# RMSNorm with repeated rows on one core: the last tile loaded by rows and stored in two halves

## Chip, cores and metric

One core of a Trainium2 chip. The metric is the device time of one execution in microseconds (us), as the median of several executions. A run's state is "slow" when its time is over 1.5% above the fastest run of the same kernel in the same call, otherwise "fast". The span of a profile is about 1.8 us shorter than the device time of the same run.

## The reference

```python
def reference(x, gamma):              # x: (8, 512, 2048) float32, gamma: (2048,)
    x_rep = np.repeat(x, 2, axis=1)   # each row twice
    rms = np.sqrt((x_rep ** 2).mean(axis=-1, keepdims=True) + 1e-6)
    return (x_rep / rms * gamma[None, None, :]).astype(np.float32)
```

4096 rows of 8 KB are read, and each normalised row is written twice: 33.6 MB in, 67.1 MB out.

## The kernel before

A tile `y` has 128 partitions, with 4 input rows (`K = 4`) and so 8 output rows (`K * R`, `R = 2`) in each. A load puts the 4 input rows into places 4 to 7; row k is normalised into place 2k and copied to 2k + 1. There are 8 tiles and 3 buffers, so load 7 waits for store 4.

```python
def load(i, eng, parts=1):
    y = rows.tile([P, K * R, D], f32, name="y")
    step = K // parts
    for k in range(0, K, step):
        at = K * (R - 1) + k
        eng.dma_start(out=y[:, at : at + step, :], in_=x_t[i, :, k : k + step, :])
    ys.append(y)

load(0, nc.scalar, parts=K)
# ... gamma, eps; loads 1 and 2, on nc.scalar
for i in range(ntiles):
    y = ys[i]
    for k in range(K):
        xk = y[:, K * (R - 1) + k, :]
        y0, y1 = y[:, R * k, :], y[:, R * k + 1, :]
        # ... tiles sq, ss, rms, rstd
        nc.scalar.activation(out=sq[:], in_=xk, func=Act.Square, accum_out=ss[:])
        nc.scalar.activation(out=rms[:], in_=ss[:], func=Act.Sqrt, scale=inv_d, bias=eps_t[:])
        nc.vector.reciprocal(out=rstd[:], in_=rms[:])
        nc.vector.scalar_tensor_tensor(out=y0, in0=xk, scalar=rstd[:], in1=gamma_b[:],
                                       op0=Alu.mult, op1=Alu.mult)
        if k == K - 1:
            nc.vector.tensor_copy(out=y1, in_=y0)
        else:
            nc.scalar.copy(out=y1, in_=y0)
    nc.sync.dma_start(out=out_t[i], in_=y.rearrange("p j d -> p (j d)"))
    if i >= 1 and i + 2 < ntiles:
        load(i + 2, nc.gpsimd)
```

Three queues feed the same 16 DMA engines: stores from SP (`nc.sync`), the first three loads from ACT (`nc.scalar`), loads 3 to 7 from POOL (`nc.gpsimd`, the "software" queue). A run is a stretch of bytes contiguous on both sides, moved as one piece. A load has 128 runs of 32 KB (4 adjacent rows), a store 128 of 64 KB; each engine gets 8 of them.

## Time and profile before

| | before |
|---|---|
| time, median of 3 runs | 244.24 us (244.11 to 244.63) |
| span of the profile | 242.7 us |
| one load run of 32 KB / store run of 64 KB on its engine | 1.213 / 2.418 us |
| load 7 landed, median engine / last engine | 202.0 / 204.1 us |
| store 6 landed, median engine / last engine | 216.5 / 218.5 us |
| DMA idle before the last store (15 of 16 engines) | 216.7 to 221.9 us |

The runs and the landings are from the trace's records of single transfers, where each of the 16 engines ends its share of a DMA with a 4-byte write to a semaphore. These records agree with the instructions' times to some 0.3 us: load 7's last engine ends at 204.1 us in the records, while the instructions see the load landed at 204.4. All times are from the start of the span.

From the page of the kernel before: the span, the engines' busy time, what the DMA moved, and the chain of work that ended last, by engine.

```profile
span 242.7 us, 307 instructions
...
DVE 88.9 (37%) x73; ACT 116.1 (48%) x122; POOL 5.3 (2%) x10
...
DMA packets 2740, 100.69 MB, mean 415 GB/s; under 512 B 305, under 2 KB 305, under 8 KB 305
...
DMA 74%; ACT 10%; DVE 5%; ACTq 1%; issue 1%; POOLq 0%; SPq 0%
```

DMA is the limit: 415 GB/s in the mean, and three quarters of the chain, while no compute engine is busy half the time. So this change looks for time where the DMA stands idle. The stretches table of the kernel before, near the end, shows where; its columns are the stretch, its length, the busy time and instructions of DVE, ACT and POOL, the clock, the DMA share and GB/s (a transfer counts whole in the stretch in which it starts, so a share can pass 1).

```profile
core 0: us, DVE busy (x) ACT busy (x) POOL busy (x), PEclk, DMA share, GB/s
...
204.00:213.00 9.00, 4.95 (x4) 8.50 (x10) 0.00 (x0) 1.00 1.07 466
213.00:217.00 4.00, 2.28 (x2) 3.84 (x5) 0.00 (x0) 1.00 0.64 279
217.00:221.00 4.00, 3.89 (x4) 1.90 (x1) 0.00 (x0) 1.00 0.00 0
221.00:225.00 4.00, 0.00 (x0) 0.00 (x0) 0.00 (x0) 1.00 1.22 524
```

The DMA thins out at 213 us, moves nothing from 217 to 221, and then carries the last store by itself. The chain of waits of the kernel before, in order of time (start, length, what), tells what it waited for:

```profile
132.22 34.69 DMA out_dram<-y
...
167.48 36.93 DMA y<-in_x_dram
...
204.43 2.01 ACT sq L71 x2
...
208.89 1.99 ACT sq L71 x2
210.87 3.59 ACT y L83 x2
...
214.89 2.35 DVE y L76
...
219.73 1.23 DVE y L81
```

Load 7 is on its way for 36.93 us, then ACT and DVE work through four rows until 220.96 us. Then the store is issued, as the timeline of the store queue shows (start, length of the issue, engine, line, operation):

```profile
221.02 0.33 SPq L84 DMA_DIRECT2D out_dram<-y  x1
```

Its first run starts at 221.9. So 16.6 us of compute stand between landing and store, and the rest of store 6 covers about 12 of them.

### The profile page before, as it was taken

How to read it: one execution, taken by the hardware profiler on the slowest of the kernel's cores; microseconds unless marked ns; L12 is line 12 of the kernel's file. 1: busy time of each engine (PE TensorE's matmuls, PEld its weight loads, DVE VectorE, ACT ScalarE, POOL GpSimd, SP SyncE). 2: the span in 40 equal slices, each digit the busy share in tenths (PEclk: the TensorE clock that was granted, in tenths of full speed). 3: DMA queues.
4: the chain of work that ended last, by engine and by line, in shares of the span. 5: the costliest groups of instructions: out<-in, count | busy, mean ns of one | idle time of the engine just before them, and what ended most of it. 6: DMA issues, size and time to landing. Idle time of an engine off the chain costs nothing.

```text
span 242.7 us, 307 instructions
## 1 busy us (share of the span) xinstructions
DVE 88.9 (37%) x73; ACT 116.1 (48%) x122; POOL 5.3 (2%) x10
## 2 busy tenths in 40 slices
DVE  0458557772000035900557007550085400864000
ACT  2994997990000079600994019920299103991000
POOL 4000000010000000000000000000000000000000
DMA  7999999999899999799799799799999898948794
GB/s 270 443 439 437 400 432 454 410 466 432 373 459 405 459 432 518 346 518 432 346 432 518 346 432 518 342 437 427 432 437 508 351 508 351 518 184 346 346 518 173
DMA packets 2740, 100.69 MB, mean 415 GB/s; under 512 B 305, under 2 KB 305, under 8 KB 305
## 3 DMA queue, kind: packets, MB, share of 16 engines
q1 hardware_dynamic: 1154, 67.12, 63.9%
q0 software_dynamic: 720, 20.97, 20.1%
q10 hardware_dynamic: 864, 12.58, 12.7%
q14 instruction: 2, 0.02, 0.0%
HBM read 33.56 MB, written 67.11 MB: 415 GB/s over the span
## 4 chain that ended last, share of the span: by engine, by line
DMA 74%; ACT 10%; DVE 5%; ACTq 1%; issue 1%; POOLq 0%; SPq 0%
DMA y<-in_x_dram 44%; DMA out_dram<-y 30%; ACT sq L71 6%; DVE y L76 4%; ACT y L83 4%; ACTq L52 1%; DVE y L81 1%; ACT rms L73 0%; DVE rstd L75 0%; POOLq L52 0%; SPq L84 0%; POOLq L112 0%
## 5 line engine op out<-in xcount | busy, mean ns | idle before, releaser
L71 ACT ACTIVATE sq<-y 128x2048 f32<-128x2048 f32 x32 | 59.7, 1866 | 95.6 <-DMA y<-in_x_dram 95.6
L76 DVE SCALAR_TENSOR_TENSOR y<-y,rstd,gamma_b 128x2048 f32<-128x2048 f32 x32 | 75.3, 2352 | 1.2
L75 DVE RECIPROCAL rstd<-rms 128x1 f32<-128x1 f32 x32 | 5.1, 160 | 129.8 <-ACT rms L73 129.8
L83 ACT COPY y<-y 128x2048 f32<-128x2048 f32 x24 | 44.6, 1889 | 2.4 <-DVE y L76 2.4
L81 DVE COPY y<-y 128x2048 f32<-128x2048 f32 x8 | 9.8, 1227 | 0.3
L73 ACT ACTIVATE rms<-ss,eps_t 128x1 f32<-128x1 f32 x32 | 9.4, 294 | 0.7
L52 POOL DMA_DIRECT2D y<-in_x_dram x5 | 2.8, 559 | 159.9 <-DMA out_dram<-y 111.8
L71 ACT ACTIVATION_READ_ACCUMULATOR sq<-y 128x1 f32 x32 | 6.0, 186 | 0.0
L71 ACT ACT_TABLE_LOAD x1 | 1.3, 1283 | 4.3 <-issue 4.3
L58 POOL PARTITION_BROADCAST gamma_b<-gamma_b x1 | 2.3, 2292 | 2.6 <-DMA gamma_b<-in_gamma_dram 2.6
L73 ACT ACT_TABLE_LOAD x1 | 1.3, 1283 | 0.0
L60 DVE MEMSET eps_t<- 128x1 f32 x1 | 0.1, 59 | 0.8 <-PEq L101 0.8
L101 POOL MEMSET const-float32-0.0<- 128x1 f32 x1 | 0.1, 99 | 0.2 <-issue 0.2
L101 POOL MEMSET const-bfloat16-1.0<- 128x1 bf16 x1 | 0.1, 101 | 0.0
L101 POOL MEMSET const-uint8-127<- 128x1 uint8 x1 | 0.1, 101 | 0.0
L101 POOL MEMSET const-float32-1.0<- 128x1 f32 x1 | 0.1, 98 | 0.0
## 6 DMA issues: line engine op xcount, KB each, us to landing
y<-in_x_dram POOLq DMA_DIRECT2D x5, 4096.0 KB, 35.6
y<-in_x_dram ACTq DMA_DIRECT2D x2, 4096.0 KB, 26.9
y<-in_x_dram ACTq DMA_DIRECT2D x4, 1024.0 KB, 7.8
out_dram<-y SPq DMA_DIRECT2D x8, 34.1
gamma_b<-in_gamma_dram SPq DMA_DIRECT2D x1, 8.0 KB
```

Of the source, the lines that this page charges most:

```text
L52: eng.dma_start(out=y[:, at : at + step, :], in_=x_t[i, :, k : k + step, :])
L58: nc.gpsimd.partition_broadcast(out_ap=gamma_b[:], in_ap=gamma_b[0:1, :])
L60: nc.vector.memset(eps_t, eps)
L71: nc.scalar.activation(out=sq[:], in_=xk, func=Act.Square, accum_out=ss[:])
L73: nc.scalar.activation(out=rms[:], in_=ss[:], func=Act.Sqrt, scale=inv_d, bias=eps_t[:])
L75: nc.vector.reciprocal(out=rstd[:], in_=rms[:])
L76: nc.vector.scalar_tensor_tensor(out=y0, in0=xk, scalar=rstd[:], in1=gamma_b[:], op0=Alu.mult, op1=Alu.mult,)
L81: nc.vector.tensor_copy(out=y1, in_=y0)
L83: nc.scalar.copy(out=y1, in_=y0)
L101: nc = _bacc.Bacc("TRN2", target_bir_lowering=False, num_devices=1)
```

## The change

The intent is to close that gap: compute on row 0 before row 3 has landed, and store the first half while the second is computed.

```diff
+    def store(i, k0, k1):
+        nc.sync.dma_start(
+            out=out_t[i, :, R * k0 * D : R * k1 * D],
+            in_=ys[i][:, R * k0 : R * k1, :].rearrange("p j d -> p (j d)"),
+        )
@@
-        nc.sync.dma_start(out=out_t[i], in_=y.rearrange("p j d -> p (j d)"))
+            if i == ntiles - 1 and k % 2 == 1:
+                store(i, k - 1, k + 1)
+        if i < ntiles - 1:
+            store(i, 0, K)
         if i >= 1 and i + 2 < ntiles:
-            load(i + 2, nc.gpsimd)
+            load(i + 2, nc.gpsimd, parts=K if i + 2 == ntiles - 1 else 1)
```

Load 7 becomes four DMAs of 8 KB runs, 32 runs on each engine; store 7 becomes two DMAs of 32 KB runs. The built order of ACT's work on the last tile also changes. Before: Square of rows 0, 1, 2, copies of rows 0 and 1, Square of row 3, copy of row 2. After: Square of rows 0 and 1, copy of row 0, Square of rows 2 and 3, and only then the copies of rows 1 and 2. (The small square roots are left out here.)

## The prediction

> **What bounds the kernel now.** The DMA. The page shows 415 GB/s over the 242.7 us span and a chain of waits that is 74% DMA; ACT is busy 48%, DVE 37%. The DMA's only large idle stretch is near the end: in the stretches table it moves 279 GB/s at 213-217 us, nothing at 217-221, and then runs full. Timeline and chain: load 7 lands at 204.4, the four rows of the last tile compute until 220.96, store 7 is issued at 221.0 and its first packet moves at 221.9. Store 6 has ended by about 216.5 on 15 engines, 218.5 on a lagging one. So 3.5 to 5.5 us could be won.
>
> **How the queues share the engines.** In the trace's packets, load 7 (8 runs of 32 KB per engine, 1.213 us each) alternates one for one with store runs of 64 KB (2.418 us). The Trainium skill, DMA: Bandwidth & Descriptors, section Queues, rings and completion order, has each engine round-robin between queues by packet, typically 9-17 descriptors. This trace agrees on the round robin but shows turns of one run; even the 4-byte semaphore write waits a turn.
>
> **What the change does.** Load 7 becomes 32 runs of 8 KB, 0.309 us each (first tile's loads), so 9.89 us instead of 9.70: +0.2. Its share per turn beside a 64 KB store falls from 33% to 11%. Counting turns from 172.5 (load 6 done): six runs of store 5 end at 188.5 with 6 load runs moved; alone until store 6 starts at about 191.7, 15 moved (row 0 landed at 189.5); row 1 lands at about 197; eight runs of store 6 end at about 213.2 with 22 moved; the rest moves alone, row 2 at 213.9, row 3 at 216.5, on the lagging engine about 2 us later: row 3 at 218.7, instead of the whole load at 204.4. The load now ends when stores 5 and 6 end, not 14 us before.
>
> **Why the first half store doesn't fill the gap.** In the built instruction order ACT copies the second output of rows 1 and 2 after the Square of row 3, which waits for row 3's load. So the first half store waits for the load that lands last: 218.7 + 0.4 + Square 1.9 + copy 1.85 = 222.9 issue, first packet 0.9 later at 223.8 (before: 221.9). The second half (row 3: rms, rstd, scale 2.35, copy 1.23) is issued at about 229, hidden under the first half's 9.7 us. Then 19.4 us of data and 1.4 us of tail: span 244.6. Gain: the time from landing to the first store packet falls from 17.5 to 5.1 us; cost: landing is 14.3 later. Net +1.9.
>
> **Predicted time: 246.0 us (+0.7%), range 243.7 to 247.9.** Chances: faster by over 2% 0.04, within 2% 0.89, slower by over 2% 0.07.
>
> **What would show it.**
> - Row 3's load lands at 216-219 us; row 0 near 190; rows 1 and 2 far apart (about 197 and 214).
> - Store 5 ends some 5 us earlier than 195; store 6 about 213 instead of 216.5.
> - First half store issued 3.5-4.5 us after row 3 lands, after its Square and a copy; DMA idle gap of about 5 us still there, some 2 us later.
> - Everything before 167 us unchanged.
>
> **What would make it wrong.** If several 8 KB runs go in one turn, the load lands near 204-210, the half stores queue behind store 6, the gap closes and the span is about 239. If short software-queue descriptors cost more than 0.31 us, or the lagging engine (1.9 us here) lags more, it is slower.

## The result, and the profile after

| | before | after |
|---|---|---|
| time, median of 4 runs each | 244.44 us | 246.79 us (246.52 to 246.96) |
| ratio of the fast runs | | 1.0095, 95% interval 1.0076 to 1.0114 |
| span | 242.7 us | 244.9 us |
| last load landed, median / last engine | 202.0 / 204.1 | 216.8 / 219.0 us |
| store 6 landed, median / last engine | 216.5 / 218.5 | 216.0 / 217.2 us |
| (first) store of the last tile issued | 221.0 | 223.2 us |
| time per engine that no record covers, from 205 us to the last byte, mean of 16 | 5.4 us | 7.2 us |
| last byte moved | 241.4 | 243.7 us |

A ratio is the mean time of one kernel's fast runs over that of the other's in the same rounds, so it is not quite the ratio of the medians quoted here.

From the page of the kernel after, the same lines as before:

```profile
span 244.9 us, 317 instructions
...
DVE 89.1 (36%) x73; ACT 116.3 (48%) x122; POOL 6.9 (3%) x13
...
DMA packets 3316, 100.69 MB, mean 411 GB/s; under 512 B 369, under 2 KB 369, under 8 KB 369
...
DMA 76%; ACT 8%; DVE 4%; another core or an unknown queue 2%; ACTq 2%; issue 1%; POOL 0%; POOLq 0%; SPq 0%
```

The same bytes, moved at 411 instead of 415 GB/s. The stretches table of the kernel after:

```profile
204.00:213.00 9.00, 0.00 (x0) 1.22 (x1) 0.00 (x0) 1.00 0.93 400
213.00:217.00 4.00, 2.52 (x2) 1.08 (x3) 0.00 (x0) 1.00 0.89 381
217.00:221.00 4.00, 0.00 (x0) 1.62 (x1) 0.00 (x0) 1.00 0.03 12
221.00:225.00 4.00, 0.00 (x0) 4.00 (x5) 0.00 (x0) 1.00 0.31 131
```

The DMA is busier ahead of 217 us (381 instead of 279 GB/s in the four us before), and the gap has moved back rather than closed: 12 GB/s at 217 to 221, and still only 131 at 221 to 225. The chain of waits of the kernel after:

```profile
168.60 43.15 DMA y<-in_x_dram
...
211.78 2.01 ACT sq L77 x2
...
214.11 5.25 another core or an unknown queue
...
219.38 2.00 ACT sq L77 x2
221.38 1.79 ACT y L89
223.17 1.80 ACTq L121
...
225.40 2.36 DVE y L82
...
227.78 1.23 DVE y L87
```

The load is on the chain for 43.15 us up to row 2, and the next 5.25 us ("another core or an unknown queue") are the wait for row 3: the chain doesn't name that DMA, but the same wait stands in ACT's timeline as 5.27 us on the load. ACT had finished row 1's Square at 196 us, yet its copy of row 1 comes only after row 3's Square, at 221 us. (The 1.80 us of `ACTq L121` are the second of two copies; ACT's timeline has both as one piece of 3.68 us.) The store queue's timeline:

```profile
223.20 0.33 SPq L56 DMA_DIRECT2D out_dram<-y  x1
...
229.07 0.33 SPq L56 DMA_DIRECT2D out_dram<-y  x1
```

The second half is issued at 229.07, while the first still moves (until 233.9), and in the records the engines then run on without a pause to 243.7. So the work on row 3, with which the chain ends, cost no time: the chain follows the store issued last and doesn't show that it queued behind the first half.

Counting in the records how many runs start in steps of about one turn shows what became of the load. All 16 engines together; in both kernels store 5 moves at first:

```
before, step 1.21 us        load 32 KB  store 64 KB
 174.6                          15          0
 175.8                           1         15
 177.0                           0          1
 178.2                          15          0
 179.4                           1         15
after, step 0.91 us         load 8 KB   store 64 KB
 174.6                           7          2
 175.5                           9         13
 176.4                           0          1
 177.3                           7          2
 178.2                           9         13
 ...   (store 5 has ended, store 6 has not begun)
 190.1                          46          0
 191.0                          48          0
```

One run of the load, one run of the store, whatever their lengths. Before, the load gets 1.213 of every 3.63 us. After, it gets 0.309 of every 2.73 us, 11%. Only in the pause between store 5 and store 6 does it have the engines to itself.

### The profile page after: what moved, and what is told of

The parts are those of the page before. It is cut to its first block, busy times and chain, and to the rows that moved or that the text cites. A ratio compares the mean times of both kernels' runs of the same rounds, so it can differ in the third digit from the quotient of the medians.

```text
span 244.9 us, 317 instructions
## 1 busy us (share of the span) xinstructions
DVE 89.1 (36%) x73; ACT 116.3 (48%) x122; POOL 6.9 (3%) x13
## 4 chain that ended last, share of the span: by engine, by line
DMA 76%; ACT 8%; DVE 4%; another core or an unknown queue 2%; ACTq 2%; issue 1%; POOL 0%; POOLq 0%; SPq 0%
DMA y<-in_x_dram 46%; DMA out_dram<-y 29%; ACT sq L77 5%; ACT y L89 3%; DVE y L82 3%; ACTq L52 1%; DVE y L87 1%; ACTq L121 1%; ACT rms L79 0%; POOL y L52 0%; DVE rstd L81 0%; POOLq L52 0%; SPq L56 0%
## 5 line engine op out<-in xcount | busy, mean ns | idle before, releaser
L52 POOL DMA_DIRECT2D y<-in_x_dram x8 | 4.4, 550 | 160.2 <-DMA out_dram<-y 160.2
```

## The experiments

The theory: **(1)** an engine gives the load queue and the store queue one run each in turn, so the load's share is set by the ratio of run lengths, and cutting load 7 to 8 KB makes it land with the last bytes of store 6 rather than 14 us earlier; **(2)** the last store can then begin only after all DMA work is done, so the gap stays. Rivals: **(a)** the half stores cost time; **(b)** four DMAs, with their semaphore writes, delay the load, not the run length; **(c)** short runs or the software queue are slow in themselves; **(d)** the order of ACT's copies alone keeps the gap open.

| run | what it is | time, median | ratio of fast runs (95%) |
|---|---|---|---|
| after | the change | 246.79 | 1.0095 (1.0076 to 1.0114) |
| e1 | row loads, one store | 253.01 | 1.0359 (1.0329 to 1.0390) |
| e2 | one load, half stores | 243.42; fast 240.17, 241.06 | no interval |
| e8 | e2 again, 5 runs | 241.09 | 0.9852 (0.9820 to 0.9884) |
| e3 | the change, last tile's copies on DVE | 247.98 | 1.0162 (1.0129 to 1.0194) |
| e4 | the change, stores 5 and 6 in 16 KB runs | 242.00 | 0.9888 (0.9826 to 0.9950) |
| e5 | the change, load as one DMA of 8 KB runs | 252.78 | 1.0328 (1.0281 to 1.0375) |
| e6 | the change, two DMAs of 16 KB runs | 248.55; fast 244.29 | no interval |
| e11 | e6 again | 249.95 | 1.0233 (1.0139 to 1.0327) |
| e7 | the change, row loads on the stores' queue | 240.19 | 0.9824 (0.9795 to 0.9854) |
| e12 | e7 again | 240.50 | 0.9831 (0.9808 to 0.9853) |
| e9 | before, load 7 on the stores' queue | 241.26 | 0.9837 (0.9747 to 0.9927) |
| e10 | before, loads 3 to 7 on the stores' queue | 241.40 | 0.9829 (0.9766 to 0.9892) |

e1 to e4 ran on one chip, e5 to e8 on a second, e9 and e10 on a third, e11 and e12 on a fourth. All gave correct results. Each run but e8 had four executions, the profiled one among them. The medians are over all of them, the ratios over the fast ones alone: e1, e4, e5, e8 and e12 had one slow execution, e2 two, e6 three. Each ratio is against the kernel before.

### e1: the row loads alone

```diff
-            if i == ntiles - 1 and k % 2 == 1:
-                store(i, k - 1, k + 1)
-        if i < ntiles - 1:
-            store(i, 0, K)
+        store(i, 0, K)
```

> The last tile's load in four rows as in the change, its store in one piece as before. Theory (each DMA engine gives the load and the store queue one run each in turn, so 8 KB runs starve beside 64 KB runs): row 3 again lands at 219 us on the lagging engine; the only store is issued when row 3 is done, at about 229 us as the second half was; first packet 0.9 later, 19.4 us of data, 1.4 of tail: span about 250.8, time about 252.5, ratio about 1.034. Rival (the load by rows helps a little and the half stores are what cost time, by their strided runs of 32 KB): faster than the changed kernel, ratio 1.00 or below.

Row 3 landed at 219.7 us on the last engine, the one store was issued at 229.8, the span was 251.5. The theory's numbers hold and rival (a) falls: without the half stores the kernel is 3.6% slower, not faster. The row loads lose, and the half stores win some of it back.

### e2 and e8: the half stores alone

```diff
-            load(i + 2, nc.gpsimd, parts=K if i + 2 == ntiles - 1 else 1)
+            load(i + 2, nc.gpsimd)
```

> The last tile's load in one piece of 32 KB runs as before, its store in two halves as in the change. Theory: load lands at 204.4 as before, the first half is issued after two copies of ACT at about 214.6, before store 6 has ended, so the DMA has no gap; 19.4 us of data from 216.5 (218.5 on the lagging engine) and 1.4 of tail: span 237.5 to 239.5, ratio 0.978 to 0.987. Rival (half stores cost time): span 243 or more, ratio 1.00 or above.

> The kernel of the half stores alone a second time, as two of its four runs were of the slow state. The load lands at about 204, no gap before the first half store; fast runs: span 237.5 to 239.5, ratio 0.978 to 0.987. If the ratio of its fast runs is above 0.99, its gain in the first call was luck.

In e2's profile (span 238.4) the load landed at 202.1 (last engine 203.3) and the first half was issued at 213.75, before store 6 ended at 216.6. The stretches table of e2 has no gap:

```profile
213.00:217.00 4.00, 2.98 (x4) 3.57 (x6) 0.00 (x0) 1.00 0.89 385
217.00:221.00 4.00, 3.19 (x2) 1.44 (x1) 0.00 (x0) 1.00 0.91 393
```

Two of e2's four executions were slow (246.79 and 245.77), so e8 repeated it: four of five fast, 240.51 to 241.30, ratio 0.9852. This part of the change is worth 1.5% by itself.

### e3: the copies off ACT, so that the first half store doesn't wait for row 3

```diff
-            if k == K - 1:
+            if k == K - 1 or i == ntiles - 1:
                 nc.vector.tensor_copy(out=y1, in_=y0)
```

> The changed kernel, but the second outputs of all rows of the last tile are copied by DVE, so that the first half store no longer waits behind row 3's Square on ACT. Theory: the first half is issued at about 200 us and begins right after store 6, at 216; but some 3.5 runs of row 3's load (6 on the lagging engine) are still to come and now take turns with runs of 32 KB, so row 3 lands at 222 to 227 instead of 219, the second half is issued about 8 us later, a gap opens between the halves: span 243 to 247.5, ratio about 1.00 to 1.02. Rival (the order of ACT's copies alone keeps the gap open): span 238 to 239.5, ratio 0.98.

The first half store was issued at 201.5 us instead of 223.2. Yet the time rose. ACT's timeline in e3, the Squares of rows 1, 2 and 3 of the last tile, with the idle time before it in brackets:

```profile
194.45 1.88 ACT L77 ACTIVATE sq<-y 128x2048 f32<-128x2048 f32 x1 [0.53 <-DMA y<-in_x_dram]
...
212.12 1.88 ACT L77 ACTIVATE sq<-y 128x2048 f32<-128x2048 f32 x1 [15.35 <-DMA y<-in_x_dram]
...
226.66 1.88 ACT L77 ACTIVATE sq<-y 128x2048 f32<-128x2048 f32 x1 [12.21 <-DMA y<-in_x_dram]
```

Row 3's Square starts at 226.66, 7.3 us later than in the change (219.38): its last runs now take turns with the first half store's 32 KB runs. On the median engine row 3 lands at 219.4, on the last at 226.3. The gap opens between the two halves instead, as the stretches table of e3 shows:

```profile
213.00:217.00 4.00, 2.48 (x2) 1.42 (x3) 0.00 (x0) 1.00 1.11 479
217.00:221.00 4.00, 0.03 (x1) 0.00 (x0) 0.00 (x0) 1.00 1.02 440
221.00:225.00 4.00, 0.00 (x0) 0.00 (x0) 0.00 (x0) 1.00 0.91 391
225.00:235.00 10.00, 4.77 (x4) 2.30 (x3) 0.00 (x0) 1.00 0.26 111
```

So rival (d) falls too. In the changed kernel the late first half even protected the load from another competitor. Moving the copies alone makes things worse (1.0162 against 1.0095, each against the kernel before; the intervals don't overlap).

### e4: shorter store runs beside the same load

```diff
-            store(i, 0, K)
+            if i >= ntiles - 3:
+                for k in range(K):
+                    store(i, k, k + 1)      # 16 KB runs
+            else:
+                store(i, 0, K)
```

> The changed kernel, with the stores of tiles 5 and 6 cut into four of 16 KB runs each; the load of the last tile is untouched, 8 KB runs from the software queue. Theory (turns of one run): a round is 0.309 + 0.61 us instead of 0.309 + 2.42, so 36 turns of the load take 33 us from about 169.5: row 3 lands at about 202 to 205 instead of 219, the half stores queue behind store 6 and the gap closes: span 237.5 to 240, ratio 0.978 to 0.987. Rival (short runs from the software queue are slow in themselves, or their issue is late): row 3 lands at 215 or later and the span is 244 or more.

Load 7 is exactly that of the change, and its competitor's runs are shorter. The edit also moves the competitor's issues, which the text of the edit hides: each row's store is issued as soon as that row is done, the first of store 5 at 156.0 us instead of 161.3, the first of store 6 at 183.0 instead of 190.9. That puts more store runs beside the load, not fewer, and leaves it no pause of its own. From 176 to 200 us the records have 419 load runs and 421 store runs, one for one. Row 3 landed at 205.2 (last engine 205.6) instead of 216.8 (219.0), and the first half store was issued at 209.9. The stretches table of e4 has no gap:

```profile
217.00:221.00 4.00, 0.00 (x0) 0.00 (x0) 0.00 (x0) 1.00 1.03 442
```

Rival (c) falls: the same short runs from the same queue land 12 us earlier on the median engine, 13 on the last. The profiled execution was slow (244.38), with one engine still moving for 3 us after the others; the three fast ones took 240.01 to 243.01, so the gain was a little below what I expected.

### e5: 8 KB runs in a single DMA

```diff
-            load(i + 2, nc.gpsimd, parts=K if i + 2 == ntiles - 1 else 1)
+            if i + 2 == ntiles - 1:
+                y = rows.tile([P, K * R, D], f32, name="y")
+                nc.gpsimd.dma_start(out=y.rearrange("p (k r) d -> p k r d", r=R)[:, :, R - 1, :],
+                                    in_=x_t[i + 2])
+                ys.append(y)
+            else:
+                load(i + 2, nc.gpsimd)
@@
-            xk = y[:, K * (R - 1) + k, :]
+            xk = y[:, R * k + R - 1 if i == ntiles - 1 else K * (R - 1) + k, :]
```

> The changed kernel with the last tile's load as one DMA again, but still in 8 KB runs: each row goes to its own output place in the tile, so the rows are not adjacent there. Tells the run length from the number of DMAs. Theory (turns of one run): 32 turns as in the change, the whole load lands at about 216.5, 219 on the lagging engine, no row earlier; the first half store is issued about 10 us later, span about 250, ratio about 1.03. Rival (it is the four DMAs and their semaphore writes that delay the load): the load lands at 204 as before, span about 239, ratio 0.98.

The load landed at 216.6 (last engine 219.0), within 0.2 us of row 3 in the change. Run length decides, and the number of DMAs doesn't: rival (b) falls. With no row early, the gap is as long as in e1 (13.6 us that no record covers from 205 us on, against 13.7 in e1 and 7.2 in the change), as the stretches table of e5 shows:

```profile
217.00:221.00 4.00, 0.00 (x0) 1.65 (x1) 0.00 (x0) 1.00 0.03 12
221.00:225.00 4.00, 3.21 (x4) 3.94 (x7) 0.00 (x0) 1.00 0.00 0
```

### e6 and e11: two DMAs of 16 KB runs

```diff
-            load(i + 2, nc.gpsimd, parts=K if i + 2 == ntiles - 1 else 1)
+            load(i + 2, nc.gpsimd, parts=2 if i + 2 == ntiles - 1 else 1)
```

> The changed kernel with the load in two DMAs of 16 KB runs. Theory by turns: 16 runs and 2 semaphore writes; six run with store 5 until 190.7, then alone until store 6's first run. If store 6 waits as in the changed kernel until about 194.2, some 12 have gone and the second pair lands at about 209.5 (211.5 on the lagging engine); if the wait is as many runs of the load as there (8), not as much time, the load is complete by about 200. In both cases the first half store is ready at 217 or before, the gap is closed or nearly: span 237.5 to 240.5, ratio 0.978 to 0.99.

> The two row pairs of 16 KB runs again, as the first profile was of the slow state: 15 engines had the second pair at 209 to 212 us as counted, but one that lagged 2.4 us at the first pair had it only at 220.7, because it had more runs left when store 6 came and each waited for a store run. If that is the cause, a profile of a fast run shows the last engine at 214 to 217 us with a lag under 2.4 us at the first pair, and a time between 240.5 and 245; if the lag is below 1 us, span 238 to 240. Rival (16 KB runs cost something else): all engines late, or a gap without a late engine.

I expected a gain and got none: e6's one fast run took 244.29, and e11 was 2.3% slower than before. The profiles say where the miss is. In e11 the second pair landed at 200.0 us on the median engine, and 15 engines had it by 208.7, but one only at 222.0. At the first pair that engine was 6.9 us late. When store 6 came it therefore had more load runs left than the others, and each of these waited for a 64 KB store run: the last engine's eight runs begin at 202.7 us, and seven of them start 3.02 us apart, a load run (0.611) and a store run (2.418). So 6.9 us of lag became 22. In e6 (slow) it was 2.5 us that became 9.1, against medians of 192.5 and 211.8. I had allowed for 2 us of lag throughout. That one late engine held the load in e11 was as expected, but its lag and its landing lay above my 2.4 us and 214 to 217 us, and the time of 249.95 us above my 240.5 to 245; why it lagged so much on that chip stays open, and so does what the one fast run of e6 did, which has no profile.

### e7 and e12: the row loads in the stores' own queue

```diff
-            load(i + 2, nc.gpsimd, parts=K if i + 2 == ntiles - 1 else 1)
+            last = i + 2 == ntiles - 1
+            load(i + 2, nc.sync if last else nc.gpsimd, parts=K if last else 1)
```

> The changed kernel with the four row loads of the last tile issued by SP on the stores' queue, between store 5 and store 6, so that no other queue takes turns with them. Theory: store 5 has the engines alone from 172.5 and ends at about 187; then the four rows land 2.5 us apart, at about 189.5, 192, 194.5 and 197 (2 us later on the lagging engine); store 6 follows them in the queue, the first half store is issued at about 203 and queues behind it, the gap is closed: span 237.5 to 239.5, ratio 0.978 to 0.987. Rival (8 KB runs are slow beside stores in any queue): rows land after 205.

> The row loads in the stores' queue again on this call's chip: rows land at about 189.5, 192, 194.5 and 197, the lagging engine up to 3 us later; slack of some 10 us between the first half store's issue and store 6's end, so a lag does not open a gap: fast runs at ratio 0.975 to 0.99.

The same four DMAs and the same half stores, but behind store 5 and ahead of store 6 in one queue: no other queue takes turns with them. The rows landed at 190.0, 192.5, 194.9 and 197.4 us, 2.5 us apart. ACT's timeline in e7 has the four Squares 0.5 to 2.4 us after the last engine's landings (190.7, 193.2, 195.7 and 198.1), the last two when ACT is free:

```profile
191.16 1.88 ACT L77 ACTIVATE sq<-y 128x2048 f32<-128x2048 f32 x1 [2.18 <-DMA y<-in_x_dram]
...
193.65 1.88 ACT L77 ACTIVATE sq<-y 128x2048 f32<-128x2048 f32 x1 [0.16 <-DMA y<-in_x_dram]
...
198.11 1.86 ACT L77 ACTIVATE sq<-y 128x2048 f32<-128x2048 f32 x1
...
200.33 1.86 ACT L77 ACTIVATE sq<-y 128x2048 f32<-128x2048 f32 x1
...
202.23 3.68 ACT L89 COPY y<-y 128x2048 f32<-128x2048 f32 x2
```

The first half store was issued at 204.1, 12.6 us before store 6 ended, and the stretches table of e7 shows no gap:

```profile
213.00:217.00 4.00, 0.00 (x0) 0.00 (x0) 0.00 (x0) 1.00 0.89 385
217.00:221.00 4.00, 0.00 (x0) 0.00 (x0) 0.00 (x0) 1.00 0.91 393
```

All four runs of e7 lay between 240.11 and 240.34; e12 repeated the ratio on another chip (0.9831), with one slow run of four.

### e9 and e10: are the pieces needed at all?

```diff
-            load(i + 2, nc.gpsimd)
+            load(i + 2, nc.sync if i + 2 == ntiles - 1 else nc.gpsimd)   # e9
+            load(i + 2, nc.sync)                                          # e10
```

(Both against the kernel before: load 7 and store 7 in one piece.)

> The kernel before with one word changed: the last tile's load, in one piece of 32 KB runs, is issued by SP on the stores' queue (between stores 5 and 6); the store stays in one piece. Theory: what matters is only that the last load has landed a full tile's compute (16.6 us) before store 6 ends. It lands at about 197 to 198, the store is issued at about 214.5, before store 6 ends at 216.5: no gap, span 238 to 239.5, ratio 0.98 to 0.987, as with the rows in that queue. Rival (the pieces are needed for the gain): ratio 0.99 or above.

> The kernel before with the loads of tiles 3 to 7 all on the stores' queue, each in one piece. Theory: each load then follows the store ahead of it in the queue without sharing; a period is 19.4 + 9.7 us as before, so nothing is won in the middle, and the end is as with only the last load there: span 237.5 to 239.5, ratio 0.978 to 0.987. The lag of one engine, 2 us by the end in the kernel before and 0.5 us with the row loads in the stores' queue, should stay below 0.7 us if it comes from the software queue. Rival (in one queue a store waits behind a load): gaps in every period, ratio above 1.

e9 has 0.9837, e10 0.9829: the same within their intervals as e7 and e8. The load landed at 197.2 in e9 on the median engine, but 201.1 on the last, so in that profile the store was issued at 218.1 and a little gap remained (span 240.9). I had expected 214.5. Two of e9's four fast executions were near that time (242.45, 242.72) and two faster (239.73, 240.07), hence its wide interval. My expectation for the lag in e10 failed: with no load on the software queue at all, the last engine was still 2.0 us behind at the last load, not under 0.7. The software queue isn't needed for that lag.

## Why the prediction was right

**Time.** 246.0 us predicted with a range of 243.7 to 247.9, 246.79 measured; span 244.6 predicted, 244.9 profiled.

**The load ends with the stores.** Row 3 was predicted at 216.5, and 218.7 on the lagging engine; it landed at 216.8 and 219.0. That turns are of one run was read from the trace before, and e4 (the other queue's runs shorter), e5 (one DMA) and e7 (one queue) show it by changing one thing each.

**The gap stays.** The first half store was predicted to be issued at 222.9, and was at 223.2. Row 3's landing to the first store run was predicted as 5.1 us and measured as 5.0 (219.0 to 224.0). The landing itself was 14.9 us later than before (14.3 predicted). The mean idle time of an engine near the end grew from 5.4 to 7.2 us. That accounts for 1.8 of the 2.3 us by which the last byte moved later; the other 0.5 is more transfer time (64.1 instead of 63.6 us per engine from 172.5 us on), of which the load's shorter runs are 0.2, as predicted.

**What was missed on the way.** I let store 6 start at 191.7, as the last store of the kernel before starts 0.9 us after its issue. It started at 194.4, 3.5 us after its issue, while the load had the engines to itself. So row 1 landed at 192.5 instead of about 197, row 2 at 199.8 on the median engine (211.4 on the last) instead of 214, and store 6 ended at 216.0 instead of about 213. The end of the load didn't move, for the engines were busy either way: the same bytes were through at the same time, whichever queue had gone first. So only the order inside was wrong. The prediction hadn't argued this; that its landing came out within 0.3 us although store 6 began 2.7 us later than it thought was luck in so far.

**What I left unsaid.** The prediction gave the order of ACT's copies as the reason why the first half store doesn't fill the gap. That is the cause of its late issue, but e3 shows that repairing it makes the kernel slower: the early half store takes turns with what is left of the load. The cause under both is the load's share: e4 and e7 keep the order of ACT's copies, and neither has a gap.

**The prediction's own doubt.** It left open that several 8 KB runs go in one turn, so that the load lands near 204 to 210. It didn't: the count of runs above has one per turn.

## What to carry to other kernels

Here, where loads and stores from different queues met on a busy DMA, cutting one side into shorter runs handed its bandwidth to the other side: look for that in your own trace by counting the turns. Before pipelining a tail by pieces, ask which transfer must land first and give that one the place, by queue order (e7, e9) or long runs, and cut the transfer that nobody waits for (e2). These edits move the same bytes, so what they could win was idle DMA time; 1.5 to 1.8% of the time was there, and moving one load to the stores' queue (e9) took as much of it, within the intervals, as any of the other cuts.

## What the Trainium skill lacked or had wrong

- *DMA: Bandwidth & Descriptors*, section "Queues, rings and completion order": the round robin between queues is right, but a turn of "≈9-17 descriptors typical" doesn't fit the runs of this kernel. Here a turn was one run of 8, 16, 32 or 64 KB (no load or store here had shorter ones), and in the kernel before load 7's 4-byte semaphore write started 2.4 us after its last run ended, after one more store run. What the page doesn't say is the consequence: the share goes by run length, and load 7's last row landed at 216.8 instead of 202.0 us on the median engine.
- The same page, section "Issuing engines are not separate DMA queues": it says that issuing from several engines only saves sequencer time. It leaves out there that the choice of queue can cost time: moving one load from POOL to SP's queue, with nothing else changed, gave a ratio of 0.9837 (e9), for there it followed store 5 instead of taking turns with it.
- The same page, section "Latency and other measured facts", gives about 0.6 us to the first byte of a DMA issued by SP or ACT. Into idle engines it was 0.9 us from the start of the 0.33 us issue, so 0.6 from its end (the kernel before, median engine, good to some 0.3 us), which agrees. What no page has: it was 3.6 to 3.8 us from the start of the issue where another queue was streaming alone, with runs of 8 KB (the change, e1, e5) as with 16 KB (e6, e11). No run shows why.
- The same section has engines 7 and 15 usually slower and, as a best guess, ties it to the software queue. Here two engines were 1.9 and 2.0 us behind the median at the last load in e10, which has no load on that queue, and one was 6.9 us behind at the first pair in e11, which has. The records don't name the engine, and the cause is open. No page says that turn-taking amplifies such a lag (6.9 to 22 us in e11).
